# Moving work of a gated recurrence's level loop from GpSimd to ScalarE and VectorE, in a two-layer encoder on one core

## The chip, the cores and the metric

The kernel runs on one core of one Trainium2 chip. The metric is the time of one execution on the device in microseconds (us), the median over several runs. A core has five engines, each with a queue of its own that it works through in order: TensorE (PE, with its weight loads as PEld), VectorE (DVE), ScalarE (ACT), GpSimd (POOL) and SyncE (SP, which only issues DMAs here). An engine that needs another's result waits on a semaphore.

## The reference

Two layers over x of 512 tokens by 1024, in float32. In each layer h = RMSNorm(x) is projected by one matrix of some 6,900 columns, whose columns belong to four groups of heads:

- A: a bidirectional gated linear recurrence (HGRN2), 4 heads of 128. For a gate z, f = sigmoid(z) in the first layer (with a lower bound in the second), the key is 1 - f, the state decays by f per channel.
- B: windowed attention with sinks. C: a bidirectional mLSTM.
- D: attention into 256 tokens of mem, which is normed by its own RMS and projected to keys and values.

Each group's output is multiplied by a gate, all four go through one output projection and are added to x. After the last layer stands a final RMSNorm. The part that this case touches is A's mixer, the norm of mem, and the start:

```python
q, k, log_f -> attn[t, s] = sum_d q[t, d] * k[s, d] * prod_{s < r <= t} f[r, d]   # and the same backwards
o = attn @ v ;  y_a = rmsnorm(o_f + o_b) * silu(z)
mem_n = mem * rsqrt(mean(mem ** 2) + 1e-6) * g
```

## The kernel before, in words

All matmuls of the projections take a value as a sum of two float32r parts, hi and lo, and run three products (hi hi, hi lo, lo hi). So each block of weights (wr, 512 rows by 256 columns, 512 KB) is loaded by SP, rounded by ACT into wh (a cast) and subtracted by DVE into wl (load_w, lines 374 to 392). wr has three buffers. proj_ch (line 435) and proj_tok (line 399) do a projection of 256 columns; results stand in PSUM banks (pj, two of them) until an evacuation by ACT or DVE.

**The order of the work.** PE's order is written by a small planner, Weave (lines 149 to 194). Projections call wv.tick with the planned time of their matmuls; a mixer is a generator that yields the PE time of its step and a latency, and its next step is emitted when the planned time has passed its due time. So a mixer's small matmuls are strewn among the projections' large ones. join runs a job's remaining steps at once. The latencies are the constants on lines 73 to 83. The order on the other engines follows a compile-time schedule that keeps to dependences and priorities.

**A's mixer** (mix_A, line 548) works for one head on the transposed layout, channels on partitions, 512 tokens along. F2 and K2 hold gate and key of both directions, Q2 the query times the gate. It builds the score matrix in levels m = 1, 2, 4, up to 64: at each level, blocks of m tokens attend to their neighbour block. For m up to 16 a level takes on PE 16 small matmuls (tile s, two PSUM banks, line 572) with an interleaved copy kc of the keys, made by `interleaved` (line 561, called at lines 574, 598 and 621: five times per head). Then K2 and Q2 are multiplied by the product tree Tm (POOL line 596, DVE line 599), DVE's copy_predicated (line 601) takes the level's scores out of the bank into ac, and DVE forms the next step of the tree, Tn (line 618). After m = 16, ac is spread into the full matrix (line 604). Before the levels stands the key sum ks (line 552), for the diagonal scores (line 576), and Q2 (line 553). Two heads run woven: group_A (line 675) is called twice per layer, so there are four A stages. A_LAT (4.3 us) is the planned latency per level.

**The start** (line 1415) loads x transposed and the first weights in pieces, makes h0 = x * g as hi and lo, and projects the first block from it, since the RMS is not there yet. Its generator rest (line 1466) sums squares on PE, computes the root (rms4, line 475), spreads it over partitions by a matmul with ones (diag and spread, lines 487 and 493) as R, and makes the normed h (norm_k, line 504). In group_A's gates (line 698) the second projection (d = 1) also takes h0 and its result is multiplied by R (`scaled`, line 705); the third (d = 0) takes h.

**mem's root** is a job of its own, mem_stats (line 1198): loads of mem (two of 512 KB), two Squares with sums on ACT, a root on DVE by a Newton iteration (rsqrt, line 357), a spreading matmul to Rm, and then mem_kv(0) (line 1217), which loads mem transposed, scales it by gain and Rm and splits it into hi and lo. It is spawned after the gates, with latencies M_LAT and M_LAT2.

Of the kernel before, what the change touches and what calls it, by code (L numbers as in the profile page):

```python
# [9 lines left out]
AF = mybir.ActivationFunctionType  # L10
# [4 lines left out]
P = 128  # L15
# [63 lines left out]
C_LAT, C_LAT1, C_LAT2 = 2000, 2600, 1350  # L79
N_LAT = 11800  # L80
D_LAT = 800
R_LAT0, R_LAT = 4000, 3500
M_LAT, M_LAT2 = 25000, 4000


def pack(inp):
# [110 lines left out]
def trunk(tc, a, dbg=None, mark=lambda s: None):  # L197
# [6 lines left out]
    with es:  # L204
# [267 lines left out]
            for c in range(n):  # L472
                gmm(ps[:, c:c + 1], sq[:, c * P:(c + 1) * P], ones[:, 0:1], first and c == 0, last)

        def rms4(ss):

            r, v, t = [sm([NC], x, 1) for x in ("rx", "rxv", "rxt")]
            act.activation(r, ss, AF.Sqrt, bias=epst, scale=1.0 / D)
            dve.tensor_scalar(v, ss, 1.0 / D, EPS, ALU.mult, ALU.add)
            dve.reciprocal(r, r)  # L480

            dve.tensor_tensor(v, v, r, ALU.mult)
            dve.scalar_tensor_tensor(t, v, -0.5, r, ALU.mult, ALU.mult)
            dve.scalar_tensor_tensor(r, t, 1.5, r, ALU.add, ALU.mult)
            return r
# [62 lines left out]
        def mix_A(l, hd, F2, K2, q, v, gz, yT):  # L548

            Q2 = u4([2, 512])  # L550
            ks = a2([512])
            gp.tensor_tensor(ks, K2[:, 0], K2[:, 1], ALU.add)
            dve.tensor_tensor(Q2, F2, V(q, 0, [[0, 2], [1, 512]]), ALU.mult)
            scr = u4([2, 512])
            at = scr[:, 1]
# [4 lines left out]

            def interleaved(lv, m):
                kc = kcs[lv % 2]
                gp.tensor_scalar(V(kc, 0, [[2 * m, 256 // m], [m, 2], [1, m]]),
                                 V(K2, 0, [[2 * m, 256 // m], [512 + m, 2], [1, m]]), 1.0, 1.0, ALU.mult, ALU.mult)
                return kc

            def per_block(n, k, qv):
# [16 lines left out]
            while m <= 64:  # L584
                k2v = V(K2, 0, [[2 * m, 256 // m], [512 + m, 2], [1, m]])
                q2v = V(Q2, 0, [[2 * m, 256 // m], [512 + m, 2], [1, m]])
                if m <= 16:
                    pl = per_block(32, lambda b: kc[:, b:b + 32],
                                   lambda b: V(Q2, b, [[2 * m, 16 // m], [512 + m, 2], [1, m]]))
                else:  # L590

                    d = lambda b: b // m % 2
                    pl = per_block(m, lambda b: K2[:, d(b), b:b + m],
                                   lambda b: Q2[:, 1 - d(b), b + m - 2 * m * d(b):b + 2 * m - 2 * m * d(b)])

                gp.tensor_tensor(k2v, k2v, V(Tm, n + 1, [[2, n // 2], [-(n + 1), 2], [0, m]]), ALU.mult)
                if 1 < m < 16:
                    kc = interleaved(lv + 1, 2 * m)
                dve.tensor_tensor(q2v, q2v, V(Tm, 1, [[2, n // 2], [n - 1, 2], [0, m]]), ALU.mult)
                if m <= 16:  # L600
                    dve.copy_predicated(ac, V(cu, lv * 32, [[0, NC], [1, 32]]), pl)
                    if m == 16:

                        gp.tensor_scalar(at.rearrange("p (c j q) -> p c j q", c=NC, j=4),
                                         V(ac, 0, [[32, NC], [0, 4], [1, 32]]), 1.0, 1.0, ALU.mult, ALU.mult)
                elif m == 32:
                    dve.copy_predicated(at.rearrange("p (c j q) -> p c j q", c=NC, j=4),
                                        V(cu, 5 * 32, [[0, NC], [32, 4], [1, 32]]), V(pl, 0, [[32, NC], [0, 4], [1, 32]]))
                else:
                    act.copy(at4[0:64, :, 64:128], pl[0:64])  # L610
                    act.copy(at4[64:128, :, 0:64], pl[64:128])

                if m == 1:
                    Tn = q
                else:
                    Tn = tot[:, toff:toff + n]
                    toff += n
                dve.tensor_tensor(Tn[:, 0:n].rearrange("p (d k) -> p d k", d=2),
                                  V(Tm, 0, [[n, 2], [2, n // 2]]), V(Tm, 1, [[n, 2], [2, n // 2]]), ALU.mult)
                if m == 1:  # L620
                    kc = interleaved(lv + 1, 2 * m)
                Tm = Tn
                n //= 2
                m *= 2
                lv += 1
                yield 560, A_LAT
# [48 lines left out]
        def group_A(l, h, pr, yT, between=None, before=None, raw=None):  # L675
# [22 lines left out]
            def gates():  # L698
                nonlocal F2, K2
                F2 = [u4([2, 512]) for _ in range(2)]  # L700
                K2 = [u4([2, 512]) for _ in range(2)]
                for d in (1, 0):
                    w = load_w(2)
                    if raw is not None and d == 1:
                        def scaled(pv, b):
                            wv.join(jobR)
                            t = a2([512])
                            dve.tensor_tensor(t, pv, R, ALU.mult)
                            ev(t, b, 1)
                        proj_ch(h0, w, [lambda pv, b=b: scaled(pv, b) for b in range(2)], bank=psc)  # L710
                    else:
                        proj_ch(h, w, [lambda pv, b=b, d=d: ev(pv, b, d) for b in range(2)])

# [16 lines left out]
            if pr == 0:  # L730
                gates()
                if raw is not None:
                    jobM.append(wv.spawn("memr", mem_stats()))
                go()
                values()
            else:
                values()
                before()
                mark(f"projA{pr}")
                gates()  # L740
                go()
# [453 lines left out]
            yield None  # L1195


        def mem_stats():

            ms = a["mem"].rearrange("b (c p) d -> p (b c) d", p=P)  # L1200
            ss = sm([2], "ssm", 1)
            ts = [u4([D]) for _ in range(2)]
            for c in range(2):
                sy.dma_start(ts[c], ms[:, c])
            yield 0, M_LAT
            for c in range(2):
                act.activation(ts[c], ts[c], AF.Square, accum_out=ss[:, c:c + 1])
            yield 0, M_LAT2
            dg = diag(rsqrt(2, ss, 1.0 / D, EPS), 2)
            yield 0, M_LAT2  # L1210
            spread(dg, Rm)
            yield 450, 1000
            mem0.append(mem_kv(0))
            next(mem0[0])
            yield 0, 0
# [199 lines left out]
        def start():  # L1415
# [22 lines left out]
            for k in range(8):  # L1438
# [19 lines left out]
                for b, pt in enumerate(pts):  # L1458
                    c = slice(b * P, (b + 1) * P)
                    mm(pt, wh[:, c], hi, start=(k == 0), stop=False)  # L1460
                    mm(pt, wh[:, c], lo, start=False, stop=False)
                    mm(pt, wl[:, c], hi, start=False, stop=(k == 7))
            es2.close()
            q = [a2([512]) for _ in range(2)]

            def rest():
# [8 lines left out]
                        dve.tensor_tensor(q[b], pts[b], R, ALU.mult)  # L1475
                for k in range(8):
                    norm_k(xs[k // 2][:, k % 2], k, R, 0, h, gp if k % 2 else dve)
                yield 900, 0
            return h, (q, h0, R, wv.spawn("R", rest(), after=R_LAT0))

        osrc = a["out"].rearrange("b (c p) d -> p (b c) d", p=P)
# [94 lines left out]
```

## Time and profile before

| What | Value |
|---|---|
| median of 3 runs | 1140.62 us (1140.06 to 1140.83) |
| the profiled execution | 1144.41 us |
| its span in the trace | 1142.6 us |
| PE busy | 1083.6 us (95%), 8886 matmuls |
| DVE busy | 809.7 us (71%) |
| ACT busy | 507.7 us (44%) |
| POOL busy | 307.4 us (27%) |
| mean granted clock of PE | 0.984 |

The rows of a profile name a line (L142 is the helper that records most operations, so there the tile names tell them apart), the engine, the operation, out<-in by tile names without numbers (u is a pool of tiles of 128x1024, a one of 128x512, pj, s, tr and o are PSUM banks), and shapes as partitions by elements. A bracket at the end of a timeline row is the idle time of the engine before it and what ended it. An instruction's time on DVE or POOL holds what it waited for inside, too.

### The profile page before, as it was taken

What the parts mean: (1) busy time and instruction counts of PE and PEld (TensorE: products, weight loads), DVE (VectorE), ACT (ScalarE), POOL (GpSimd) and SP (SyncE); (2) the same over time, 40 slices, a digit from 0 to 9 for tenths busy, and PEclk for the clock granted to TensorE, in tenths of its full rate; (3) what the DMA queues carried; (4) which work ended last, traced back from release to release, by engine and by line L of the source; (5) the groups of instructions that cost most, each with busy time, mean ns of one, the idle gap of its engine ahead of it and who ended that gap; (6) DMA issues with size and microseconds to landing.
All of it is one profiled execution on the core that took longest, in us unless ns stands there. A gap on an engine that the chain in (4) does not pass through costs nothing.

```text
span 1142.6 us, 22411 instructions
## 1 busy us (share of the span) xinstructions
PE 1083.6 (95%) x8886; PEld 973.3 (85%) x8886; DVE 809.7 (71%) x1756; ACT 507.7 (44%) x1089; POOL 307.4 (27%) x332
## 2 busy tenths in 40 slices
PE   6979999989999999999999899999898999999997
PEld 4878988989788797888788799889887787989997
DVE  7898546697586868767373785387859759588664
ACT  5614346656324434334564224376652243442443
POOL 4582000231472214011020661012308601230200
PEclk9999999999999999999999899999999999999999
DMA  6312234111211445322443221222121232362211
GB/s 213 136 56 95 75 111 130 59 58 56 93 57 57 125 98 142 120 89 93 129 136 123 75 76 57 92 64 68 41 75 57 75 106 89 97 207 75 75 38 74
DMA packets 34784, 105.42 MB, mean 92 GB/s; under 512 B 4360, under 2 KB 7816, under 8 KB 34680
## 3 DMA queue, kind: packets, MB, share of 16 engines
q1 hardware_dynamic: 33960, 101.57, 28.3%
q0 software_dynamic: 720, 2.42, 0.5%
q8 instruction: 70, 1.15, 0.4%
q14 instruction: 34, 0.28, 0.1%
HBM read 99.72 MB, written 4.26 MB: 91 GB/s over the span
## 4 chain that ended last, share of the span: by engine, by line
PE 66%; DVE 22%; issue 5%; ACT 5%; DMA 2%; POOL 1%; SPq 0%; DVEq 0%; ACTq 0%; POOLq 0%
PE pj L248 31%; PE pj L251 20%; DVE a L142 8%; DVE u L142 6%; DVE wl L142 4%; PE o L248 4%; PE s L248 4%; ACT wh L142 2%; PE s L251 2%; ACT u L142 1%; PE tr L859 1%; ACT a L142 1%; PE o L251 1%; DMA u<-in_memT 1%; DVE rq_t L142 1%
## 5 line engine op out<-in xcount | busy, mean ns | idle before, releaser
L251 PE MATMUL pj<-wh,u 128*128 128x256 f32 x1984 | 395.1, 290 | 2.6 <-ACT u L142 1.2
L248 PE MATMUL pj<-u,wh 128*128 128x512 f32 (+1 forms) x1216 | 376.2, 390 | 2.0 <-ACT a L142 1.4
L251 PEld LDWEIGHTS pj<-wh,u 128*128 128x128 f32 x1984 | 321.1, 192 | 7.0 <-ACT u L142 1.6
L142 DVE TENSOR_TENSOR wl<-wr,wh 128x1024 fp32r<-128x1024 f32 (+1 forms) x162 | 207.1, 1279 | 134.1 <-ACT wh L142 133.4
L251 PE MATMUL pj<-wl,u 128*128 128x256 f32 x992 | 282.9, 285 | 0.0
L248 PEld LDWEIGHTS pj<-u,wh 128*128 128x128 f32 x1216 | 219.0, 190 | 44.8 <-ACT a L142 2.2
L142 ACT CAST wh<-wr 128x1024 fp32r<-128x1024 f32 (+1 forms) x162 | 164.3, 1014 | 199.4 <-PE pj L248 97.7
L248 PE MATMUL pj<-u,wl 128*128 128x512 f32 (+1 forms) x608 | 233.8, 384 | 1.8 <-DVE wl L142 1.8
L251 PEld LDWEIGHTS pj<-wl,u 128*128 128x128 f32 x992 | 191.2, 193 | 0.8 <-issue 0.3
L248 PEld LDWEIGHTS pj<-u,wl 128*128 128x128 f32 x608 | 115.1, 189 | 24.6 <-DVE wl L142 2.0
L142 POOL TENSOR_TENSOR u<-u,a 128x512 f32<-128x512 f32 (+1 forms) x64 | 91.6, 1433 | 63.6 <-DVE a L142 28.9
L142 POOL TENSOR_SCALAR u<-u,rB 128x256 f32<-128x256 f32 (+1 forms) x64 | 37.4, 599 | 229.4 <-DVE rB L142 136.3
L142 DVE TENSOR_TENSOR u<-u,a 128x512 f32<-128x512 f32 (+1 forms) x56 | 61.9, 1105 | 13.0 <-PE s L251 11.0
L248 PE MATMUL pj<-wh,u 128*128 128x256 f32 (+1 forms) x320 | 62.8, 287 | 0.0
L251 PE MATMUL s<-u,u 128*32 128x32 f32 (+2 forms) x1760 | 35.1, 208 | 22.2 <-DVE a L142 19.0
L251 PEld LDWEIGHTS s<-u,u 128*32 128x32 f32 (+1 forms) x1760 | 27.5, 116 | 33.0 <-issue 19.9
L248 PE MATMUL o<-u,u 128*128 128x129 f32 (+1 forms) x384 | 51.4, 278 | 1.9 <-DVE dnC L142 1.9
L248 PEld LDWEIGHTS o<-u,u 128*128 128x128 f32 x384 | 49.1, 194 | 4.7 <-issue 2.4
L142 POOL TENSOR_TENSOR u<-u,cf 128x512 f32<-128x512 f32 x16 | 24.8, 1549 | 104.3 <-DMA u<-rdr 55.1
L142 POOL TENSOR_TENSOR u<-u,u 128x512 f32<-128x512 f32 x16 | 30.0, 1874 | 84.3 <-DVE u L142 51.2
L248 PEld LDWEIGHTS pj<-wh,u 128*128 128x128 f32 x320 | 50.9, 188 | 0.7 <-issue 0.5
L142 POOL TENSOR_TENSOR a<-u 128x512 f32<-128x512 f32 x12 | 21.9, 1822 | 106.3 <-DVE u L142 70.6
(211 smaller groups left out, 1563.1 us busy)
## 6 DMA issues: line engine op xcount, KB each, us to landing
wr<-in_wpk SPq DMA_DIRECT2D x154, 512.0 KB, 3.3
u<-in_xT SPq DMA_DIRECT2D x16, 256.0 KB, 5.0
u<-rdr SPq DMA_DIRECT2D x16, 256.0 KB, 4.6
u<-gdr SPq DMA_DIRECT2D x16, 192.0 KB, 5.4
u<-in_memT SPq DMA_DIRECT2D x4, 512.0 KB
xd<-u POOLq DMA_DIRECT2D x4, 512.0 KB, 5.0
u<-xd SPq DMA_DIRECT2D x4, 512.0 KB, 4.6
out<-u SPq DMA_DIRECT2D x8, 256.0 KB, 2.0
```

The lines of the kernel that those rows point to most:

```text
L142: r = f(*args, **kw)
L248: nc.tensor.matmul(out, l, r, start=start, stop=stop)
L251: nc.tensor.matmul(out, l, r, start=start, stop=stop, skip_group_check=True)
L859: nc.tensor.transpose(pt[:, j * P:(j + 1) * P], pr[e][:, j * P:(j + 1) * P], ident)
```

## The change

In A's mixer, the five interleaved key copies of each head and the spread of ac go from POOL to ACT, and the key sum goes from POOL to DVE. The key update (line 596) stays on POOL, the update of Q2 and the tree stay on DVE. mem's root is computed in the step that makes R and h: its loads are issued at the end of the start, its Squares, a Sqrt by rms4 and the diagonal come behind the norm of x, and its spread a step later. What is left of the old job makes mem's scaled copy, 20 us (planned) after the gates. The third projection takes h0 too, and its result is multiplied by R; its bank stays pj. Three planner constants change.

```diff
-R_LAT0, R_LAT = 4000, 3500
-M_LAT, M_LAT2 = 25000, 4000
+R_LAT0, R_LAT = 6000, 3500
+M_LAT, M_LAT2 = 20000, 2500
...
-        def rms4(ss):
-
-            r, v, t = [sm([NC], x, 1) for x in ("rx", "rxv", "rxt")]
+        def rms4(ss, n=NC):
+
+            r, v, t = [sm([n], f"{x}{n}", 1) for x in ("rx", "rxv", "rxt")]
...
-            gp.tensor_tensor(ks, K2[:, 0], K2[:, 1], ALU.add)
+            dve.tensor_tensor(ks, K2[:, 0], K2[:, 1], ALU.add)
...
-                gp.tensor_scalar(V(kc, 0, [[2 * m, 256 // m], [m, 2], [1, m]]),
-                                 V(K2, 0, [[2 * m, 256 // m], [512 + m, 2], [1, m]]), 1.0, 1.0, ALU.mult, ALU.mult)
+                act.copy(V(kc, 0, [[2 * m, 256 // m], [m, 2], [1, m]]), V(K2, 0, [[2 * m, 256 // m], [512 + m, 2], [1, m]]))
...
-                        gp.tensor_scalar(at.rearrange("p (c j q) -> p c j q", c=NC, j=4),
-                                         V(ac, 0, [[32, NC], [0, 4], [1, 32]]), 1.0, 1.0, ALU.mult, ALU.mult)
+                        act.copy(at.rearrange("p (c j q) -> p c j q", c=NC, j=4), V(ac, 0, [[32, NC], [0, 4], [1, 32]]))
...
-                    if raw is not None and d == 1:
-                        def scaled(pv, b):
+                    if raw is not None:
+                        def scaled(pv, b, d):
                             wv.join(jobR)
                             t = a2([512])
                             dve.tensor_tensor(t, pv, R, ALU.mult)
-                            ev(t, b, 1)
-                        proj_ch(h0, w, [lambda pv, b=b: scaled(pv, b) for b in range(2)], bank=psc)
+                            ev(t, b, d)
+                        proj_ch(h0, w, [lambda pv, b=b, d=d: scaled(pv, b, d) for b in range(2)], bank=psc if d else pj)
...
-                    jobM.append(wv.spawn("memr", mem_stats()))
+                    jobM.append(wv.spawn("memn", mem_norm(), after=M_LAT))
...
-        def mem_stats():
-
-            ms = a["mem"].rearrange("b (c p) d -> p (b c) d", p=P)
-            ss = sm([2], "ssm", 1)
-            ts = [u4([D]) for _ in range(2)]
-            for c in range(2):
-                sy.dma_start(ts[c], ms[:, c])
-            yield 0, M_LAT
-            for c in range(2):
-                act.activation(ts[c], ts[c], AF.Square, accum_out=ss[:, c:c + 1])
-            yield 0, M_LAT2
-            dg = diag(rsqrt(2, ss, 1.0 / D, EPS), 2)
-            yield 0, M_LAT2
-            spread(dg, Rm)
-            yield 450, 1000
+        def mem_norm():
+            yield 0, 0
             mem0.append(mem_kv(0))
             next(mem0[0])
             yield 0, 0
...
+            ms = a["mem"].rearrange("b (c p) d -> p (b c) d", p=P)
+            ssm = sm([2], "ssm", 1)
+            mt = [u4([D]) for _ in range(2)]
             es2.close()
+            for c in range(2):
+                sy.dma_start(mt[c], ms[:, c])
             q = [a2([512]) for _ in range(2)]
...
-                yield 900, 0
+                for c in range(2):
+                    act.activation(mt[c], mt[c], AF.Square, accum_out=ssm[:, c:c + 1])
+                dg = diag(rms4(ssm, 2), 2)
+                yield 900, M_LAT2
+                spread(dg, Rm)
+                yield 450, 0
```

## Rows read from the trace of the kernel before

**Rows 1.** PE's waits over the span: for whom, us in total, times, longest us
```profile
PE s L251 <- DVE a L142: 19.0, 11, 4.1
```

**Rows 2.** Timeline of PE: start us, us, instruction, idle before; the long waits
```profile
64.51 0.54 PE L251 MATMUL s<-u,u 128*32 128x32 f32 x32 [4.12 <-DVE a L142]
...
313.28 0.54 PE L251 MATMUL s<-u,u 128*32 128x32 f32 x32 [2.25 <-DVE a L142]
...
650.51 0.66 PE L251 MATMUL s<-u,u 128*32 128x32 f32 x32 [3.39 <-DVE a L142]
...
874.29 0.61 PE L251 MATMUL s<-u,u 128*32 128x32 f32 x32 [3.30 <-DVE a L142]
```

**Rows 3.** Stretches: us, busy PE, PEld, DVE, ACT, POOL, PEclk, DMA share, GB/s
```profile
64.50:69.50 5.00, 4.99 (x56) 4.84 (x56) 4.93 (x7) 0.00 (x0) 4.75 (x4) 0.66 0.16 61
313.20:318.70 5.50, 5.42 (x89) 5.21 (x89) 5.43 (x7) 0.29 (x1) 5.25 (x4) 0.69 0.01 3
650.50:656.50 6.00, 5.99 (x80) 5.80 (x84) 5.93 (x8) 0.10 (x1) 5.75 (x5) 0.55 0.01 3
874.20:878.20 4.00, 3.91 (x49) 3.88 (x50) 3.93 (x5) 0.00 (x0) 3.75 (x4) 0.57 0.00 0
...
640.00:675.00 35.00, 30.67 (x543) 28.92 (x542) 34.12 (x40) 6.78 (x10) 29.29 (x21) 0.90 0.19 62
```

**Rows 4.** Timeline of DVE in the third A stage
```profile
632.61 1.22 DVE L142 TENSOR_TENSOR wl<-wr,wh 128x1024 fp32r<-128x1024 f32 x1 [3.50 <-ACT wh L142]
...
644.06 2.14 DVE L142 TENSOR_TENSOR wl<-wr,wh 128x1024 fp32r<-128x1024 f32 x1
...
647.38 2.84 DVE L142 TENSOR_TENSOR u<-u,u 128x512 f32<-128x512 f32 x1
650.08 0.28 DVE L142 COPY_PREDICATED a<-cu,s 128x128 f32<-128x128 uint8 x1
...
660.58 0.68 DVE L142 TENSOR_TENSOR u<-u,a 128x512 f32<-128x512 f32 x1
```

**Rows 5.** Timeline of POOL, a key update late in the first stage
```profile
95.57 1.08 POOL L142 TENSOR_TENSOR u<-u,a 128x512 f32<-128x512 f32 x1 [0.98 <-PE s L251]
```

**Rows 6.** POOL's groups by form: count | busy us, mean ns | idle before us
```profile
L142 POOL TENSOR_TENSOR u<-u,a 128x512 f32<-128x512 f32 x48 | 74.4, 1550 | 23.0 <-PE s L251 20.3
L142 POOL TENSOR_SCALAR u<-u 128x512 f32<-128x512 f32 x42 | 43.1, 1027 | 19.9 <-DVE u L142 19.2
...
L142 POOL TENSOR_TENSOR a<-u 128x512 f32<-128x512 f32 x12 | 21.9, 1822 | 106.3 <-DVE u L142 70.6 <-ACT u L142 35.1 <-DMA u<-in_xT 0.7
```

**Rows 7.** ACT's groups by form: a cast of weights, a copy out of SBUF
```profile
L142 ACT CAST wh<-wr 128x1024 fp32r<-128x1024 f32 x154 | 161.1, 1047 | 195.2 <-PE pj L248 97.7 <-PE pj L251 62.6 <-issue 28.4
...
L142 ACT CAST u<-a 128x512 fp32r<-128x512 f32 x8 | 5.0, 619 | 9.5 <-DVE a L142 9.5
```

**Rows 8.** Timeline of DVE, mem's root in the first stage: first and last of 12
```profile
55.71 1.26 DVE L142 TENSOR_SCALAR rq_v<-ssm 128x2 f32<-128x2 f32 x1
...
61.32 0.16 DVE L142 SCALAR_TENSOR_TENSOR rq_y<-rq_t,rq_y 128x2 f32<-128x2 f32 x1
```

**Rows 9.** DMA issues of the page: count, KB each, median us to landing
```profile
wr<-in_wpk SPq DMA_DIRECT2D x154, 512.0 KB, 3.3
```

**Rows 10.** Timeline of PE between 24 and 46 us: its two waits
```profile
24.82 1.02 PE L251 MATMUL tr<-ones,a 128*128 128x1 f32 x8 [1.71 <-DVE a L142]
44.95 0.50 PE L248 MATMUL pj<-u,wh 128*128 128x512 f32 x1 [0.36 <-DVE u L142]
```

**Rows 11.** DVE's groups by form: the scalings of mem, both layers
```profile
L142 DVE SCALAR_TENSOR_TENSOR u<-u,pg,Rm 128x256 f32<-128x256 f32 x16 | 6.8, 478 | 2.3 <-DMA u<-in_memT 2.3
```

**Rows 12.** The chain that ended last: start us, us, what
```profile
665.19 3.02 PE pj L251 x24
```

**Rows 13.** Timeline of ACT at the first Sigmoid
```profile
43.30 1.28 ACT L142 ACT_TABLE_LOAD   x1
44.59 0.63 ACT L142 ACTIVATE u<-a 128x512 f32<-128x512 f32 x1
```

## The prediction

> **What bounds the kernel now.** I read the busy shares first (the table above), then whom TensorE (PE) waits for, then the order of time around those waits, then the engine that releases them. PE is busy 95% of the span and no other engine comes near, so the change can only pay where PE stands idle or slow. The list of PE's waits has one entry that stands out: the small score matmuls of the A mixer (tile s, line 251) wait 11 times for a VectorE (DVE) instruction on tile a, 19.0 us together [rows 1]. In order of time they sit in the four A stages, two heads each. Every stage has one long wait at the same point, the second head's first level: 4.12, 2.25, 3.39 and 3.30 us, together 13.1 us [rows 2]; the seven others share the remaining 5.9. What comes behind the long wait costs half as much again: in the stretch after it the granted clock averages 0.66, 0.69, 0.55 and 0.57 [rows 3], between the levels of 1.2 and 2.4 GHz. A stretch of 5.0 us at 0.66 loses 5.0 x 0.34 = 1.7 us; the other three lose 5.5 x 0.31 = 1.7, 6.0 x 0.45 = 2.7 and 4.0 x 0.43 = 1.7, together 7.8. So the four stages hold 13.1 + 7.8 + 5.9 = 26.8 us that PE could give back. The rest of PE's time is matmul work that the change leaves alone.
>
> **Why PE waits there.** The tile s has two banks. The second head's first-level scores need the bank that the first head's copy_predicated frees, and that instruction sits on DVE behind three others: the subtraction for wl, the product tree's first step and the update of Q2. In the third stage the first of these starts at 644.06 and takes 2.14 us, the last takes 2.84, and copy_predicated starts at 650.08, 6.0 us after the first began [rows 4]. Elsewhere the same wl form takes 1.22, and a product of 128x512 like the 2.84 one takes 0.68 [rows 4]. GpSimd (POOL) is busy through all that time: 29.29 of 35 us in this stage, with DVE at 34.12 and ScalarE (ACT) at 6.78 [rows 3]. POOL's two-input product takes 1.08 us where DVE leaves it alone [rows 5] and 1.55 in the mean [rows 6]. So the two engines stretch each other, and the long waits are DVE instructions stretched by POOL's queue.
>
> **The change, part by part.**
>
> Key copies and spreads. Five interleaved copies per head, 8 heads, are 40 POOL instructions; the group of 42 (two belong to B) has a mean of 1.03 us [rows 6], so some 41 us leave POOL, 10 per stage. On ACT one should take what a copy of 128x512 out of SBUF takes there, 0.62 us [rows 7]: with the 8 spreads 48 x 0.62 = 30 us, 7.4 per stage. That lies beside a PE stage of 30 to 38 us in which ACT is used for 6.78 of 35 [rows 3]: cost zero while ACT keeps up. The fine stride of the first copies has no row on ACT. Its lower bound is 0.62; a plain doubling, 1.24, is my upper one, an estimate, since no row has it. I take 0.62, because DVE's strided and plain products take the same 0.68 [rows 4]. Even 1.24 would leave ACT half free.
>
> Key sums. Eight POOL adds with a mean of 1.82 us [rows 6] become eight DVE adds of 0.68 [rows 4]: 1.4 us of DVE per stage, ahead of the critical copy_predicated. What they displace on POOL stood in front of the whole chain.
>
> Together, in the third stage: from the first head's key sum to the second head's first key update POOL now runs six instructions (sum, copy and update of each), afterwards two. DVE's three instructions ahead of copy_predicated need 1.22 + 0.68 + 0.68 = 2.6 us undisturbed, plus 1.4 for the sums, plus at most one POOL product of 1.08: 5.1 against the 6.0 of before [rows 4, 5]. DVE also starts them earlier, because what lies ahead of them is no longer stretched. The wait of 3.39 us goes if DVE is 3.4 us earlier: 0.9 from here, the rest from the earlier start. I leave 0.5 us of waiting in each of the third and fourth stages, where layer 1's two gate scalings also stand on DVE, and take it that so short a wait does not lower the clock. So the first waits give 13.1 - 1.0 = 12.1 and the clock 7.8. Of the seven later waits I take half, 3.0: POOL's load per level falls from two products and two copies to two products, but DVE's small tree products still share with POOL.
>
> Mem's root. Twelve small DVE instructions run from 55.71 to 61.48 in the first stage, right ahead of its long wait; the first takes 1.26 us, the last 0.16 [rows 8]. They leave the stage, so that wait of 4.12 has two causes removed. In place of them come a Sqrt on ACT, five small DVE operations and a diagonal, beside the second and third projections, with two Squares on ACT and the two loads of mem, issued on SP's queue ahead of the second projection's weights. These weights are there early and their subtraction waits for DVE, so the loads cost nothing; without that cover they would cost up to two landings of 512 KB, 2 x 3.3 us [rows 9]. SP waits for no buffer at these two DMAs. The spreading matmul now stands early in PE's order: if its diagonal is late, PE waits, and the projection is queued behind it. The nearest row is the wait of x's sums of squares, 1.71 us [rows 10]; the bounds are 0 and 1.7, and I take 0.5.
>
> Mem's scaled copy starts 20 us after the gates instead of some 34: eight scalings at 0.48 us [rows 11] and two subtractions of at most 2.14 each [rows 4], 6 to 8 us of DVE, move into the middle of the first stage's levels. Bounds: 0, if the freed time covers them, and one more long wait of 4.1 + 1.7. I take 1.0.
>
> Third projection. It needs no normed h, so PE's wait of 0.36 us [rows 10] goes. Two products on DVE come (1.4 us), on the way to the second gate's sigmoid; the time of the twelve that left covers them. The planner's other constants move no instruction that has a price of its own.
>
> **Sum.** 12.1 + 7.8 + 3.0 + 0.4 - 0.5 - 1.0 = 21.8 us. The profiled execution took 1144.4 (span 1142.6 and 1.8 around it), 3.8 over the median of 1140.6; the saving is made of waits, so I take it off the median: 1118.8.
>
> **Rivals.**
>
> Half of it. POOL's key update and DVE's tree stay and still stretch each other. Then the long waits halve (6.5), the clock still falls in two of four stages (3.9 kept of 7.8) and the later waits stay: 10.4 us, 1130. For it: DVE is at 34.12 of 35 us in the stage [rows 3]. Against: POOL loses half its instructions. The Trainium skill, GPSIMD Engine Reference, Specifications, says that the SBUF interfaces are shared with VectorE for DVE instructions with two SBUF inputs; by that rule the key sum contends on either engine and this case gains weight. Chance 0.20.
>
> ACT's order becomes the bound, and it is slower. A key copy waits on ACT for POOL's update, and the cast of weights and the evacuation of pj stand behind it. One block is 1.55 + 0.62 + 1.05 [rows 6, 7] = 3.2 us, and 3.8 with an evacuation priced as the copy. PE comes back to the same bank after 24 matmuls, 3.0 us [rows 12]. Beyond that point PE waits: 0.8 us at each of some 6 evacuations (one per 48 matmuls, 6 us, in some 35) in 4 stages is 19 us; as a late key copy also holds up the scores themselves, only the 10.4 us of the case above is saved: 19 - 10.4 = +8.6, 1149. Against it: ACT has the time, and copies seldom meet a late update. Chance 0.06.
>
> A table switch. Were mem's Sqrt to come behind the first Sigmoid on ACT, two more loads of 1.28 us [rows 13] would delay the gates by 2.6: 1121. The Trainium skill, ScalarE: Activation LUTs, What ACT_TABLE_LOAD costs, adds a drain of 1.38 to each; the row shows the next activation right after the load, so I don't take the 5.3 us it would give. Chance 0.07.
>
> Nothing happens: DVE is late for other reasons, the weight subtractions, and POOL only looks busy. 1140.6. Against it is the 2.84 beside the 0.68 [rows 4]. Chance 0.05.
>
> **How the numbers follow.** Forecast 0.62, and the cases above. The forecast's best end takes all of 26.8, 0.4 and the 1.7 at the sums of squares: 28.9, about 1111. Its worst end loses the bounds of mem: some 1128. The half case, 1130, with the bounds of mem's copy beside it (1.0 taken, 5.8 at most) reaches past 1133. So 1111 to 1133 holds about 0.85. Faster by over 0.2% (about what a measurement of this kernel tells from no change, 2.3 us): 0.62 + 0.20 + 0.07 = 0.89; same 0.05; slower 0.06.
>
> **What would show it.** Right: the waits of s for DVE on tile a fall from 19.0 to under 5 us, the clock stays full in the four stages, the Q2 update ahead of the first copy_predicated takes near 0.7, POOL's busy time falls by some 55 us or more and ACT's rises by some 30. Wrong: waits of pj for ACT, a clock that still falls behind the second head's first level, more table loads than before, or PE waiting for mem's diagonal before 50 us.

## The result, and the profile after

The changed kernel takes 1136.2 us in the median, the kernel before 1142.05 in the same comparison: a ratio of 0.9946 (95% interval 0.9928 to 0.9964). It is faster by 0.5%, some 6 us. The forecast was 21.8 us and a range of 1111 to 1133, so the sign was right and the size was not. The profiled execution took 1137.1 us (span 1135.3; before 1144.4 and 1142.6), so the two profiles, 7.3 us apart, are fit to be read against each other.

The first part of the page after, busy time by engine:

```profile
PE 1079.4 (95%) x8886; PEld 968.2 (85%) x8886; DVE 795.3 (70%) x1759; ACT 538.3 (47%) x1138; POOL 243.4 (21%) x276
```

POOL lost 64.0 us and ACT gained 30.6 (it had 307.4 and 507.7): the work went where the change sends it. What did not follow stands in the list of PE's waits (for whom, us in total, times, longest):

```profile
PE s L251 <- DVE a L142: 13.6, 10, 3.4
...
PE tr L248 <- DVE a L142: 3.2, 2, 3.0
```

The first line answers [rows 1]: 19.0 us became 13.6, not "under 5". The second is new. In order of time, PE's waits in the four A stages and ahead of the first:

```profile
25.66 1.02 PE L251 MATMUL tr<-ones,a 128*128 128x1 f32 x8 [1.89 <-DVE a L142]
...
47.01 0.67 PE L248 MATMUL tr<-a,ones 128*128 128x256 f32 x2 [2.99 <-DVE a L142]
...
67.18 0.54 PE L251 MATMUL s<-u,u 128*32 128x32 f32 x32 [1.12 <-DVE a L142]
...
79.88 0.46 PE L251 MATMUL s<-u,u 128*32 128x32 f32 x32 [3.38 <-DVE a L142]
...
86.26 0.60 PE L251 MATMUL s<-u,u 128*32 128x32 f32 x32 [0.90 <-DVE a L142]
...
91.70 0.36 PE L251 MATMUL pj<-wh,u 128*128 128x256 f32 x1 [1.03 <-DVE u L142]
...
327.68 0.46 PE L251 MATMUL s<-u,u 128*32 128x32 f32 x32 [1.60 <-DVE a L142]
...
648.45 0.54 PE L251 MATMUL s<-u,u 128*32 128x32 f32 x32 [1.72 <-DVE a L142]
...
661.79 0.46 PE L251 MATMUL s<-u,u 128*32 128x32 f32 x32 [1.60 <-DVE a L142]
...
868.76 0.54 PE L251 MATMUL s<-u,u 128*32 128x32 f32 x32 [1.79 <-DVE a L142]
```

The long waits of [rows 2] are now 1.12, none, 1.72 and 1.79: 13.1 us became 4.6. But the waits late in the levels grew, and a wait of 2.99 us for mem's diagonal stands at 47.01, in the projection that waited 0.36 before [rows 10]. The stretches that answer [rows 3], and two of the start (us, busy PE, PEld, DVE, ACT, POOL, granted clock, DMA share, GB/s):

```profile
67.10:72.10 5.00, 4.92 (x96) 4.72 (x97) 4.93 (x7) 2.53 (x5) 3.61 (x3) 1.00 0.83 279
648.40:654.40 6.00, 5.95 (x133) 5.57 (x133) 5.93 (x8) 2.51 (x5) 4.63 (x3) 1.00 0.13 51
868.70:872.70 4.00, 3.94 (x52) 3.91 (x53) 3.93 (x7) 2.03 (x5) 2.63 (x2) 0.68 0.17 69
640.00:675.00 35.00, 31.28 (x590) 29.10 (x589) 31.39 (x45) 13.60 (x21) 14.90 (x9) 1.00 0.24 77
...
26.00:32.00 6.00, 6.00 (x22) 4.56 (x22) 2.81 (x12) 1.97 (x4) 0.00 (x0) 0.72 0.46 132
46.00:52.00 6.00, 4.99 (x15) 4.02 (x16) 3.06 (x5) 4.25 (x7) 0.00 (x0) 0.72 0.28 87
```

The clock (2.4 GHz at 1.00, 1.2 at 0.50) falls behind only one of the long waits any more, but twice in the start, where it was 1.00 before. Set side by side by stage, from PE's timeline (a stage runs from its first diagonal scores to the key transposes; idle is the sum of its bracketed waits; clock is the time lost to it, 1 minus the granted clock, summed over slices of 2 us):

| | start until first scores | stage 1 | stage 2 | stage 3 | stage 4 |
|---|---|---|---|---|---|
| before: us | 57.55 | 47.00 | 44.53 | 45.88 | 45.53 |
| before: idle / clock | | 5.7 / 1.7 | 3.9 / 1.7 | 4.3 / 3.4 | 5.0 / 1.7 |
| after: us | 63.23 | 46.65 | 41.50 | 43.37 | 43.22 |
| after: idle / clock | | 6.4 / 0 | 1.9 / 0 | 3.7 / 0 | 2.6 / 1.7 |

The start loses 5.7 us in this pair of profiles; stages 2 to 4 gain 2.3 to 3.0 each; stage 1 gains next to nothing. The other 4.8 us of the 7.3 lie between the stages and behind the last, where either profile can be 1 to 3 us off (the way from stage 2 to stage 3 takes 291.6 us before, 291.0 after, and 288.5 in the first kernel below).

**What holds the levels.** VectorE's timeline in the third stage of the changed kernel:

```profile
637.79 2.91 DVE L142 TENSOR_TENSOR wl<-wr,wh 128x1024 fp32r<-128x1024 f32 x1 [0.34 <-ACT wh L142]
...
643.70 2.85 DVE L142 TENSOR_TENSOR wl<-wr,wh 128x1024 fp32r<-128x1024 f32 x1 [0.41 <-ACT wh L142]
646.47 0.68 DVE L142 TENSOR_TENSOR a<-u 128x512 f32<-128x512 f32 x1
647.08 1.08 DVE L142 TENSOR_TENSOR u<-u,u 128x512 f32<-128x512 f32 x1
648.01 0.29 DVE L142 COPY_PREDICATED a<-cu,s 128x128 f32<-128x128 uint8 x1
```

and POOL's in the same time, whole:

```profile
637.58 2.04 POOL L142 TENSOR_TENSOR u<-u,u 128x512 f32<-128x512 f32 x1 [46.87 <-DVE a L142]
643.43 2.04 POOL L142 TENSOR_TENSOR u<-u,u 128x512 f32<-128x512 f32 x1 [3.80 <-ACT u L142]
```

The Q2 update now takes 1.08 instead of 2.84 [rows 4]. But each of the two key updates starts just ahead of a wl, and that wl takes 2.9 instead of 1.22: POOL's second product ends at 643.43 + 2.04 = 645.47, wl 1.08 later. The Trainium skill has this as a rule (SBUF — State Buffer, Who interferes with whom): a VectorE instruction with two SBUF inputs and a GpSimd one that reads SBUF exclude each other, and the second to issue waits for the whole of the first. This row agrees to within 0.2 us.

**What holds the start.** VectorE after, ahead of mem's diagonal:

```profile
27.69 0.26 DVE L142 SCALAR_TENSOR_TENSOR rx<-rxt,rx 128x4 f32<-128x4 f32 x2
...
33.16 5.80 DVE L142 TENSOR_TENSOR a<-u,a 128x512 f32<-128x512 f32 x4
38.88 1.21 DVE L142 TENSOR_TENSOR wl<-wr,wh 128x1024 fp32r<-128x1024 f32 x1
40.02 4.71 DVE L142 SCALAR_TENSOR_TENSOR u<-a,pg,u 128x512 fp32r<-128x512 f32 x7
44.66 1.21 DVE L142 TENSOR_TENSOR wl<-wr,wh 128x1024 fp32r<-128x1024 f32 x1
45.80 0.74 DVE L142 SCALAR_TENSOR_TENSOR u<-a,pg,u 128x512 fp32r<-128x512 f32 x1
46.46 0.41 DVE L142 TENSOR_TENSOR a<-cf,rx 128x256 f32<-128x256 f32 x1
```

Both roots are ready at 27.95. The last row is mem's diagonal: it stands in DVE's order behind the whole normed copy of h, 18.5 us later, and the spreading matmul that needs it stands early in PE's.

### The profile page after: what moved, and what is told of

It is laid out like the page before. It is cut to its first block, busy times and chain, and to the rows that moved or that the text cites. A ratio compares the mean times of both kernels' runs of the same rounds, so it can differ in the third digit from the quotient of the medians.

```text
span 1135.3 us, 22387 instructions
## 1 busy us (share of the span) xinstructions
PE 1079.4 (95%) x8886; PEld 968.2 (85%) x8886; DVE 795.3 (70%) x1759; ACT 538.3 (47%) x1138; POOL 243.4 (21%) x276
## 4 chain that ended last, share of the span: by engine, by line
PE 71%; DVE 18%; ACT 3%; issue 2%; DMA 1%; POOL 0%; SPq 0%; DVEq 0%; ACTq 0%; POOLq 0%
PE pj L248 33%; PE pj L251 23%; DVE a L142 7%; DVE u L142 5%; PE o L248 4%; DVE wl L142 3%; PE s L248 3%; PE s L251 2%; ACT wh L142 1%; PE tr L857 1%; PE o L251 1%; ACT u L142 1%; ACT a L142 1%; DVE rq_t L142 1%; PE tr L1290 1%
## 5 line engine op out<-in xcount | busy, mean ns | idle before, releaser
L251 PE MATMUL pj<-wh,u 128*128 128x256 f32 x1984 | 390.7, 287 | 3.2 <-ACT u L142 1.2
L251 PEld LDWEIGHTS pj<-wh,u 128*128 128x128 f32 x1984 | 317.0, 190 | 8.2 <-ACT u L142 2.4
L142 DVE TENSOR_TENSOR wl<-wr,wh 128x1024 fp32r<-128x1024 f32 (+1 forms) x162 | 215.4, 1330 | 135.8 <-ACT wh L142 135.3
L251 PEld LDWEIGHTS pj<-wl,u 128*128 128x128 f32 x992 | 188.3, 190 | 0.8 <-issue 0.3
L142 DVE TENSOR_TENSOR u<-u,a 128x512 f32<-128x512 f32 (+1 forms) x56 | 50.2, 897 | 15.9 <-PE s L251 13.5
L248 PEld LDWEIGHTS pj<-wh,u 128*128 128x128 f32 x320 | 51.0, 188 | 0.7 <-issue 0.5
L251 PE MATMUL s<-u,u 128*32 128x32 f32 (+2 forms) x1760 | 35.0, 207 | 17.2 <-DVE a L142 13.6
L142 ACT COPY u<-u 128x512 f32<-128x512 f32 x40 | 27.0, 684 | 40.7 <-DVE u L142 22.8
L248 PE MATMUL pj<-wl,u 128*128 128x256 f32 (+1 forms) x160 | 45.3, 283 | 0.0
```

The lines of the kernel that those rows point to most:

```text
L142: r = f(*args, **kw)
L248: nc.tensor.matmul(out, l, r, start=start, stop=stop)
L251: nc.tensor.matmul(out, l, r, start=start, stop=stop, skip_group_check=True)
```

## The experiments

One per cent is 11.4 us. Differences are taken from the ratios to the kernel before.

**The two halves of the change.** The first kernel is the one before with the three hunks of mix_A alone; the second is the changed one with those three undone.

```diff
-            gp.tensor_tensor(ks, K2[:, 0], K2[:, 1], ALU.add)
+            dve.tensor_tensor(ks, K2[:, 0], K2[:, 1], ALU.add)
...
-                gp.tensor_scalar(V(kc, 0, ...
+                act.copy(V(kc, 0, ...
...
-                        gp.tensor_scalar(at.rearrange(...
+                        act.copy(at.rearrange(...
```

> Only stage A's three moves (key copies and block spreads to ScalarE, key sums to VectorE); the start, mem's root and the third projection stay as before. Theory (the stages gain, the start loses): the first diagonal scores come where they came before, at 57.6 us in the span, no wait above 0.3 us stands between 25 and 50 us beyond those of before, each of the three later stages gains 2 to 3 us, and the time is 9 to 11 us under the kernel before, about 1132. Rival (A's moves bring nothing by themselves, the 5.9 us come from elsewhere): within 2 us of before.

> The reverse: mem's root with that of x and the third projection from raw h, with stage A's three moves undone. Theory: the first diagonal scores come some 5.7 us later than before, at 63.2 us, with waits of TensorE near 25.7 us (about 1.9) and near 47 us (about 3.0) and the clock lower behind each; some of it is given back by the time stage 1 ends, and the time is 3 to 8 us over the kernel before (1145 to 1150). Rival (the start costs nothing in the end): at or under the kernel before.

Stage A's moves alone: 0.9888 (0.9868 to 0.9908), 12.8 us under before. The first scores come at 57.70, stages 1 to 4 take 44.32, 41.47, 43.44 and 43.27. The rest alone: 1.0041 (1.0024 to 1.0059), 4.7 us over before, first scores at 63.12, with waits of 1.88 and 2.79 us in the start. Both theories hold in the main, and both rivals fall; together the halves make 8.1 us where the change made 6.2, and their intervals allow for that. Three things were not expected. A's moves gave a little more than the 9 to 11 us. In the second kernel the clock fell only behind the first of the two waits (0.52 in 26 to 32 us, 1.00 from 34 us to the first scores). And its stage 1 became longer, 51.17 against 47.00, and only the way to stage 2 gives 3.6 of it back. So the change is two opposite effects, and the question is why the first is 12.8 and not 22.9 (the forecast's 12.1 + 7.8 + 3.0), and where the second comes from.

**Which of A's moves.** The kernel before, with the hunks for the copies and spreads only, and with the hunk for the key sum only.

> The kernel before, with the key copies and block spreads on ScalarE, and the key sums left on GpSimd. Theory (the key copies with their 40 GpSimd instructions stand beside VectorE's products and carry most of the gain): 70 to 100 per cent of the 13 us of both moves, 1130 to 1134. Rival (the key sum, ahead of the first copy in GpSimd's queue and in the chain of the first level, carries it): under 4 us.

> The kernel before, with the key sums on VectorE and the copies and spreads left on GpSimd. Theory: it gains 0 to 4 us, since the first copy then starts some 1.5 us sooner on GpSimd, but the update still stands behind a GpSimd product. Rival: 8 us or more, the chain of the first level being the one that counts.

0.9915 (0.9901 to 0.9929), 9.7 us, for the copies, and 0.9972 (0.9960 to 0.9984), 3.2 us, for the sums: three quarters and one quarter, and together the 12.8.

**What is left in the levels.** Two kernels built on A's moves alone. The first leaves out POOL's key updates of widths 1 to 8 (the later levels work on keys that were not updated); the second lets POOL form the same products into a tile that the level does not read.

```diff
-                gp.tensor_tensor(k2v, k2v, V(Tm, ...), ALU.mult)
+                if m >= 16:
+                    gp.tensor_tensor(k2v, k2v, V(Tm, ...), ALU.mult)
```

```diff
-                gp.tensor_tensor(k2v, k2v, V(Tm, ...), ALU.mult)
+                ko = k2v if m >= 16 else V(at, 0, [[2 * m, 256 // m], [m, 2], [1, m]])
+                gp.tensor_tensor(ko, k2v, V(Tm, ...), ALU.mult)
```

> The kernel with stage A's moves alone, without GpSimd's key updates of the levels of width 1 to 8 (32 products left out in all; later levels work on keys that were not updated). Theory (what still holds the level's update on VectorE is a GpSimd product beside a VectorE product, mostly the weights' low part): wl beside the second head's first level takes 1.2 us in place of 3.0, the two waits of 1.6 to 1.9 us of each stage go, and the time is 6 to 12 us under that kernel. Rival (VectorE's own amount of work sets the waits): the waits stay at 1.6 to 1.9 us, the time moves by under 3 us.

> The same kernel, but GpSimd forms the 32 products of the same shape into a tile that the level does not read, so that they stand at the same place in its queue, and nobody waits for them until the level of width 16. Theory (the two engines hold each other up whenever their products run together, whoever reads the result): wl beside it takes 3.0 us again, and the time is within 3 us of the kernel with stage A's moves alone, 5 us or more over the one without the products. Rival (the level waits for the updated keys, through ScalarE's copy): it is as fast as the one without the products.

0.9758 (0.9739 to 0.9777) without the products, 14.8 us under A's moves alone where the theory had 6 to 12, and 0.9877 (0.9861 to 0.9894) with them aside, where A's moves alone had 0.9888. 13.6 us come back as soon as POOL does the work, though nobody in the level reads it. That rules out the way over the updated keys and ScalarE's copy. PE's wait list has "s <- DVE a" at 12.7 us with A's moves alone, 0.3 without the products, 10.7 with them aside. VectorE around the second head's first level, without them:

```profile
630.99 1.22 DVE L142 TENSOR_TENSOR wl<-wr,wh 128x1024 fp32r<-128x1024 f32 x1 [2.05 <-ACT wh L142]
632.13 0.68 DVE L142 TENSOR_TENSOR a<-u 128x512 f32<-128x512 f32 x1
632.73 1.12 DVE L142 TENSOR_TENSOR u<-u,u 128x512 f32<-128x512 f32 x1
633.69 0.31 DVE L142 COPY_PREDICATED a<-cu,s 128x128 f32<-128x128 uint8 x1
```

and with them aside, POOL's product first:

```profile
633.48 3.54 POOL L142 TENSOR_TENSOR u<-u,u 128x512 f32<-128x512 f32 x1 [2.68 <-DVE u L142]
...
635.63 2.48 DVE L142 TENSOR_TENSOR wl<-wr,wh 128x1024 fp32r<-128x1024 f32 x1 [0.56 <-ACT wh L142]
638.03 0.68 DVE L142 TENSOR_TENSOR a<-u 128x512 f32<-128x512 f32 x1
638.63 1.07 DVE L142 TENSOR_TENSOR u<-u,u 128x512 f32<-128x512 f32 x1
639.56 0.29 DVE L142 COPY_PREDICATED a<-cu,s 128x128 f32<-128x128 uint8 x1
```

wl is 2.48 rather than the 3.0 expected: wl starts later within POOL's product, which ends at 633.48 + 3.54 = 637.02, and again ends 1.09 us after it. Of these four VectorE instructions it is the only one that is stretched. The Q2 update takes 1.1 us even undisturbed. Over the span VectorE's busy time is 752.4 us without the 32 products and 791.2 with them: each costs VectorE 1.2 us.

**The key updates on VectorE.** That price says what to do. On A's moves alone, the updates of widths 1 to 16, and in the second kernel of width 1 only, go to VectorE, last in the level's order (the edit of the first; the second has m == 1 in place of m <= 16).

```diff
-                gp.tensor_tensor(k2v, k2v, V(Tm, ...), ALU.mult)
-                if 1 < m < 16:
+                if not (m <= 16):
+                    gp.tensor_tensor(k2v, k2v, V(Tm, ...), ALU.mult)
+                if 1 < m < 16 and not (m <= 16):
                     kc = interleaved(lv + 1, 2 * m)
...
-                if m == 1:
+                if m <= 16:
+                    dve.tensor_tensor(k2v, k2v, V(Tm, ...), ALU.mult)
+                if m == 1 or (1 < m < 16 and (m <= 16)):
                     kc = interleaved(lv + 1, 2 * m)
```

> The kernel with stage A's moves alone, with the key updates of the levels of width 1 to 16 (40 products) on VectorE, behind the level's query update, selection and product of the decays, so that no GpSimd product stands beside VectorE's. Theory (a GpSimd product costs VectorE more than the product itself would: leaving 32 of them out took 38.8 us off VectorE's busy time, 1.2 us each, against 0.7 to 1.1 us for the same product on VectorE): 6 to 13 us under the kernel with the moves alone, 1117 to 1123. Rival (VectorE becomes the bound of the levels with 40 more products): within 2 us of it, or over it.

> The same with only the 8 key updates of the level of width 1 on VectorE. Theory (the first wait of each stage, 1.9 to 2.3 us, comes from this product beside wl): that wait goes, the later one of 1.6 us stays; 4 to 8 us under the kernel with the moves alone. Rival (the chain of the first level is as long either way, since the next key copy waits for an update that now comes last): within 2 us.

0.9769 (0.9745 to 0.9792), 13.6 us under A's moves alone, just past the theory's 6 to 13, and 0.9847 (0.9826 to 0.9867), 4.7 us under. The first beats both the kernel before and the changed one, 1115.25 us in the median. In the second the first wait of stage 1 fell from 2.34 to 0.51 us and the later one stayed at 1.61, as expected. Two of VectorE's groups by form in the first (count, busy us, mean ns, idle before):

```profile
L142 DVE TENSOR_TENSOR wl<-wr,wh 128x1024 fp32r<-128x1024 f32 x154 | 197.1, 1280 | 128.9 <-ACT wh L142 128.2
L142 DVE TENSOR_TENSOR u<-u,a 128x512 f32<-128x512 f32 x80 | 55.0, 697 | 17.9 <-PE s L251 17.6
```

The 32 updates of widths 2 to 16 are in the second line, 80 instructions at 697 ns; with A's moves alone 48 of the same form took 841, and wl 1379. With 40 products more, VectorE is busy for less: 777.3 us against 793.4 with A's moves alone.

**The start.** First, mem's squares, root and diagonal ahead of the normed copy of h, with the spread right behind that of x; then the same with the due time of x's root as before; and on A's moves alone, the third projection from raw h and nothing else of the start.

```diff
+                    for c in range(2):
+                        act.activation(mt[c], mt[c], AF.Square, accum_out=ssm[:, c:c + 1])
+                    dgm = diag(rms4(ssm, 2), 2)
                 yield 900, R_LAT
                 with tc.high_priority():
                     spread(dg, R)
+                    spread(dgm, Rm)
...
-R_LAT0, R_LAT = 6000, 3500
+R_LAT0, R_LAT = 4000, 3500
```

> The changed kernel, with mem's squares, root and diagonal formed ahead of the normed copy of h on VectorE, and mem's spreading matmul right behind that of x on TensorE. Theory (VectorE's order keeps the diagonal back): the 2.99 us wait at 47 us and the clock's fall behind it go, the first diagonal scores come 4 to 5 us earlier, at about 58.5 us, and the time is 3 to 5 us under the changed kernel, about 1132. Rival (VectorE is the bound of the start, and its work only changes places): the first diagonal scores stay at 62 to 63 us and the time stays within 1 us of the changed kernel.

> The changed kernel with mem's diagonal formed ahead of the normed copy of h, and x's sum of squares and root due as early as before (4000 ns in place of 6000). Theory (that later due time lets a weights' low part stand ahead of the last square sum, TensorE waits 1.9 us and its clock then falls): no clock under 0.9 between 26 and 34 us, the first diagonal scores at 57 to 59 us, and 2 to 4 us under the kernel with the early diagonal alone. Rival (the fall of the clock comes from the loads of mem or from something else in the start): the clock is again near 0.5 at 28 us and the time within 1 us.

> The kernel with stage A's moves alone, and the third projection from raw h, with mem's root and all the constants as before. Theory (this part is worth the 0.38 us wait at 45.1 us that it takes away, and the two copies scaled by x's root on VectorE): between 0.5 us under and 1.5 us over the kernel with the moves alone. Rival (it is this part that loses the 5.7 us of the start): 3 us or more over.

The early diagonal gives 0.9919 (0.9902 to 0.9936), 3.1 us under the changed kernel, with intervals that overlap a little. The wait at 47 us is gone and the clock of 46 to 52 us is 1.00. The first scores come at 60.58 and not at 58.5; in that profile the first fall of the clock was deeper, 3.4 us by the sum of the table above where the changed kernel lost 1.7:

```profile
26.00:32.00 6.00, 5.90 (x18) 5.06 (x19) 3.35 (x14) 1.38 (x3) 0.00 (x0) 0.52 0.34 119
46.00:52.00 6.00, 6.00 (x28) 4.84 (x27) 4.85 (x7) 5.77 (x8) 0.00 (x0) 1.00 0.26 87
```

The due time of x's root: 0.9905 (0.9887 to 0.9923), 1.6 us more, which the intervals do not separate; both mends together are 4.7 us under the changed kernel, with intervals apart. The first wait fell to 1.72 us and the first scores came at 58.27, yet the clock of 26 to 32 us was 0.72 as in the changed kernel. So that theory is not borne out. The third projection alone: 0.9901 (0.9884 to 0.9918), 1.5 us over A's moves alone and inside both intervals. Its 0.38 us wait went, the first scores came 1.5 us earlier, and the first level's wait became 4.23 us where it was 2.34.

Side by side, all profiles tell where the start's loss lies. With both mends and a clock loss of 1.7 us ahead of them the first scores come at 58.27, 58.49 and 58.99 us (three kernels); with mem's root where it was before and the same clock loss, at 58.87, 58.88 and 58.91 (three others). So with its diagonal early, mem's root costs the start nothing that these profiles show. Of the 5.7 us between the two profiles above, 1.7 is the fall of the clock at 26 us, which kernels without mem's root in the start have too; the rest belongs to the wait for mem's diagonal and the clock behind it.

**Mem's scaled copies in stage 1.** They stand among the levels in the changed kernel. One kernel has them due far later (on the changed kernel), one somewhat later (on the one with the two mends of the start).

```diff
-M_LAT, M_LAT2 = 20000, 2500
+M_LAT, M_LAT2 = 34000, 2500
...
-M_LAT, M_LAT2 = 20000, 2500
+M_LAT, M_LAT2 = 28000, 2500
```

> The changed kernel, with mem's scaled copies due after stage 1's levels, in place of among them. Theory (mem's scaled copies on VectorE hold up stage 1's updates): the waits at 79.9, 86.3 and 91.7 us (3.38, 0.90 and 1.03 us) shrink to under 1.5 us in sum, and the time is 3 to 5 us under the changed kernel. Rival (the waits are those of the levels' own work, or the copies are only moved to where they hold up something else): the waits stay, or a new wait for mem's copies stands ahead of the projections of mem, and the time stays within 1 us.

> The changed kernel with mem's diagonal early, x's root as early as before, and mem's scaled copies due at 28000 ns in place of 20000, behind most of stage 1's levels, where they stood before. Theory (the 3.39 us and 1.04 us waits in stage 1 belong to mem's copies, and the kernel with stage A's moves alone, whose mem copies stand there, has all that the change can give): stage 1 takes 44 to 45 us in place of 47.7, nothing over 2 us is given back before stage 2, and the time is 2 to 4 us under the kernel with these two mends, 1128 to 1130. Rival (given back, as it was with 34000, where the way to stage 2 became 9.7 us longer): within 1 us or over.

Far later: 0.9962 (0.9949 to 0.9975), no gain. Stage 1 took 42.12 us, 4.5 less, and the way to stage 2 took 211.24 instead of 201.55, with a wait of 5.0 us for ScalarE in it. Somewhat later: 0.9920 (0.9906 to 0.9935), against 0.9905 no gain either; stage 1 took 44.34, as the theory said, and the way to stage 2 205.17 instead of 201.45. The rival holds in both: at these places the cost moves and does not go away. Neither put the copies where they stood before, as the expectation has it: VectorE's scalings of mem run from 91.3 to 107.2 us in the first and from 87.5 to 98.9 in the second, in the last levels of stage 1; in the kernel before they ran from 103.8 to 108.5, at its end, and with A's moves alone from 99.9 to 104.9. That place was not tried with the new start.

**The changed kernel with the key updates on VectorE**, as it is, and with all the mends.

> The changed kernel as it is, with the key updates of the levels of width 1 to 16 on VectorE. Theory (GpSimd's key updates beside VectorE's products are what the forecast counted as gone with the copies): 11 to 14 us under the changed kernel, 1122 to 1125, and none of the waits of 1.6 to 1.8 us in stages 2 to 4. Rival (in the changed kernel the start and mem's copies set the time, so that it gains only a part): 6 us or less.

> The same with the key updates of the levels of width 1 to 16 on VectorE. Theory (the two mends lie in different places and add up): 12 to 15 us under the kernel without the key updates moved, 1113 to 1117, and no clear difference from stage A's moves with the key updates moved (1115). Rival (with VectorE's 40 products more, mem's copies become a bound of stage 1): 1119 or more.

0.9785 (0.9771 to 0.9800): 18.4 us under the changed kernel, more than the theory's 11 to 14. Most of the difference lies in stage 1, which went from 46.65 to 39.57 us with mem's copies still among its levels; the others went to 39.11, 39.43 and 39.19. The line "s <- DVE a" is no longer in PE's wait list. Stage 1 of this kernel as one stretch:

```profile
63.20:102.80 39.60, 39.50 (x734) 36.81 (x733) 39.08 (x96) 20.10 (x33) 5.33 (x4) 1.00 0.29 95
```

VectorE is busy for 39.08 of 39.60 us, a larger share than the 34.12 of 35 in [rows 3], and PE has no wait there. So mem's copies hold stage 1 up only beside POOL's products. With the mends of the start and of mem's place besides: 0.9763 (0.9748 to 0.9779), 2.5 us less, which the intervals don't quite separate. The theory's 1113 to 1117 holds (1116.2 in the median); the step to it is 18 us under the same kernel with POOL's updates, not 12 to 15.

## Why the forecast was right in its sign and wrong in its size

**Right.** PE's waits for VectorE in the A stages were what could be gained, and POOL's work beside VectorE's made them: without 32 of its products the line is 0.3 us. POOL fell by 64 us, ACT rose by 30.6 at 684 ns a copy (0.62 taken), and ScalarE did not become the bound: the waits of pj for it are short in both kernels (3.0 us in all after, 3.4 before). No more table loads, 12 before and after. The wait of the third projection went.

**First waits, 12.1 forecast, 8.4 found (13.1 to 4.6).** The step that failed is "at most one POOL product of 1.08 ... DVE also starts them earlier". In the third stage the way from wl's start to copy_predicated shrank from 6.02 to 4.31 us, even more than the 5.1 of the forecast, and those 1.71 us are what the wait lost, 3.39 to 1.72. The earlier start, which was to bring the other 2.5, never came: wl started 0.22 us ahead of the stage's first scores before and 0.18 after. The first head's key update sits on the wl before it (2.91 us at 637.79) as the second head's sits on this one. I counted one product of 1.08, a row of a late level [rows 5]; there are two, and at width 1 each takes 2.04. And 0.68, a product of a later level in [rows 4], is not the undisturbed Q2 update, which takes 1.1 at this stride.

**Clock, 7.8 forecast, 6.5 found** on the stretches of [rows 3] (only the fourth stage still falls, 0.32 x 4.0 = 1.3). The kind was right. The waits of 0.5 us that the forecast left, "so short" that they lower no clock, did not come about; what was left was longer, and behind 1.79 us in stage 4 the clock fell, behind 1.72 in stage 3 it did not. Behind a wait of 0.51, in stage 1 of the kernel with the updates of width 1 on VectorE, it did not fall either.

**Later waits, 3.0 gain forecast, 3.1 loss found (5.9 to 9.0)**, by size the step that failed most. The fall "from two products and two copies to two products" halves a count, but the products left still lie beside VectorE's. Ahead of the 1.60 us at 661.79:

```profile
657.88 1.98 DVE L142 TENSOR_TENSOR wl<-wr,wh 128x1024 fp32r<-128x1024 f32 x1
659.78 1.65 DVE L142 TENSOR_TENSOR u<-u,a 128x512 f32<-128x512 f32 x1
...
657.59 4.80 POOL L142 TENSOR_TENSOR u<-u,a 128x512 f32<-128x512 f32 x3 [0.67 <-ACT u L142]
```

Beside three key updates wl takes 1.98 in place of 1.22, and the Q2 update 1.65 in place of 0.68: 1.7 us more. With A's moves alone the later waits are 6.6 us (12.7 less first waits of 2.34, none, 1.86 and 1.87), so A's moves lose 0.7 there where they were to gain 3.0, and the other 2.4 come from stage 1, where mem's scaled copies share the queue, with 3.38 and 0.90 us.

**Mem's spread, 0.5 taken, bounds 0 to 1.7; found 2.99 and 1.7 of clock behind it**, 3.1 us in the timed runs. (In the kernel with the start's part alone the wait is 2.79 and the clock behind it stays full.) The bound was wrong because I took it from the nearest wait of the same kind, and did not write down what stands ahead of the diagonal on DVE. The text followed the loads past SP's queue and the Sqrt past ACT's, but not the diagonal past DVE's.

**Mem's scaled copies, 1.0 taken, bounds 0 to 5.8.** Waits of 3.38, 0.90 and 1.03 us stand there; 1.60 of the first stands in stages without the copies too, so they add some 3.7, between the bounds (the first two are in the later waits above already). Part is given back on the way to stage 2, 2.1 us shorter than before (3.6 of 4.2 in the kernel without A's moves), and the two later places tried gain nothing. With POOL's products gone they hold nobody up.

**The rival "half of it"** (10.4 us) named the mechanism that holds, POOL's key update and VectorE's products stretching each other, and the size: A's moves alone gave 12.8, with the first waits halved (13.1 to 6.1), the later ones about as they were (5.9 to 6.6), and the clock falling in one stage where it had two. It had 0.20, with the rule of the Trainium skill beside it (GPSIMD Engine Reference, Specifications: the interfaces are shared for VectorE instructions with two SBUF inputs). Read with the stretched wl of the kernel before, that rule should have made it the likeliest. With the start's loss on top the result fell beyond the range.

Open is what makes the clock fall at 26 us, and whether mem's copies at the end of stage 1, with the root early, would bring back the 1.9 us (inside the intervals) by which the changed kernel with both mends of the start stays over A's moves alone.

## What to carry to other kernels

Where two engines shut each other out, do not count instructions that leave; list which instruction of the one lies beside which of the other after the change, and charge the whole duration of the first at each meeting. An instruction that costs the neighbour more than it would cost there (1.2 against 0.7 to 1.1 us here) belongs on the neighbour, even if that one is busy 99% of the stage. And follow every moved instruction past the queue of each engine it uses, down to the small one that releases the matmul.

## What was not expected of the hardware

PE's wait for x's sums of squares, near 25 us, was 1.70 to 1.91 us in all 17 profiles. Behind it the granted clock of 26 to 32 us was 1.00 in 5 of them (waits of 1.71, 1.73, 1.74, 1.89 and 1.90 us) and 0.50 to 0.78 in the mean in the other 12 (1.70 to 1.91). The length of the wait does not tell the two apart. All 8 profiles with mem's root moved to the start are among the 12, but so are 4 of the 9 others, so its cause is not settled. At other places it is the same: a wait of 2.79 us at 48.47 in the kernel with the start's part alone lowered no clock, and one of 1.79 in stage 4 of the changed kernel did.

On ScalarE the copy with the finest interleave took 0.87 us (632.35 in the kernel with A's moves alone), a later one 0.62: the forecast took 0.62 and put the upper bound at 1.24.
